# A hybrid attention and pooling layer on one core: a second buffer for the output weights' pieces, and other places for three kinds of small steps

## The chip, the core and the metric

The kernel runs on one core of a Trainium2 chip. The metric is the device time of one execution in microseconds; the time before is the median of three runs, 1445.88 us. One more execution was profiled, and all rows of a profile that are shown come from it. The engines are named as the profile names them: PE multiplies matrices (its weight loads are PEld), DVE does elementwise work and reductions, ACT copies and applies functions, POOL is a slower elementwise engine, and SP only issues transfers. SP and POOL issue nearly all DMA transfers here, each from a queue of its own that is worked off in order.

## The reference

The layer takes x (1024 tokens by 2048 channels) and does, in float32:

```
h = x @ w_in + b_in                       # 2048 -> 4352 columns: q, k, v, g_attn, u_pool, g_pool
a = banded_sink_attention(q, k, v) * silu(g_attn)   # 16 heads of 64, 2 key heads, window 128,
                                          # blocks of 128 queries against 256 keys,
                                          # with a bias by distance and a learned sink per head
b = multiscale_pool(u_pool) * silu(g_pool)          # trailing means over 2, 4, 8, 16 tokens, a map per group
mix = concat(a, b) @ w_out                # 2048 -> 2048
ple = sigmoid(x @ w_gate_ple) * (p @ w_ple)
out = layer_norm(2 ** 0.25 * x + mix + ple)         # gain and bias per channel
```

## The kernel before, in words

**Products.** All large products run as three matmuls in a reduced float format (`mm3`, lines 180 to 185: high part times high part, high times low, low times high). A *job* makes two blocks of 128 output columns, for one half of the inner dimension of 2048. It uses seven products instead of eight (p1 to p7, line 47), on sums and differences of quarters of the weights and of the activations. One product is 12 matmuls of 128x512: 4 chunks by three. The weights of a job come as two raw pieces of 512 KB into a ring of five buffers (`raw`, `feed_raw`, line 194). For each product ACT casts a quarter to its high part (`wh`, line 816) and DVE takes the low part (`wl`, `lo`, line 131), up to four products ahead.

**Gathering.** Products accumulate in PSUM banks `qa` and `qb`, two buffers each. In a job that runs alone the order is p1, p2, p6, p5, p7, p3, p4 (operands b11, b21, t2, t1, t3, b22, t4). p1, p6, p7 and p4 share one `qa` bank, so that what a product left there has to be read before a later one may add to it: ACT copies it out (`part`, line 423) or DVE adds it (`part`, line 425). Only the product between the two covers that reading.

**Stages.** Stage 1 makes q, k, v from the first half of the inner dimension, stage 2 (from about 150 us to 700 us) from the second, and then the second half of all other columns. The attention runs inside stage 2, beside the products. Stage 3 takes the first half of the other columns and applies the gates, stage 4 and 5 are the output projection, and the layer norm ends the kernel.

**Places.** After each product the clock of the program moves by one *tick* (`tick`, line 162). Small steps are put at ticks: `after(n, step)` places a step n ticks from now, `later(n, step)` does so too, and besides puts its instructions, on each engine, behind the last gathering that was placed there. A planner with costs of its own then settles the order on each engine, and an engine never leaves that order. So the places set what stands in front of what on PE, ACT, DVE, POOL and SP.

**Attention.** `heads` (line 575) handles four heads and two blocks of 128 queries; sixteen such units start 9 ticks apart. Counted from its start, a unit loads queries and its two bias tiles at 0 (`s<-q`, `s<-in_rel`, line 593), splits the queries at 3, makes scores at 6 and 10 (`score`: 8 matmuls of line 613, then 4 reductions on DVE, line 616), the shift at 9 and 13, exponentials at 10 and 14, their scaling at 12 and 16, transposes at 15 and 19 (`trans`, line 649, one `tr` bank), and products with the values at 21 and 25 (`value`: 4 matmuls of line 665 into a `pv` bank, a copy on ACT, line 669, and two additions on DVE, line 672). Its tiles come from a pool of 15 buffers of 2 KB per partition (`slots0`, line 1285).

**Centring the output weights.** Beside all this `centre_weights` (line 937) loads the output weights twice in 64 pieces of 256 KB into `cw`, a pool of one buffer (line 1087). In the first pass DVE reduces each piece to sums (`wsum`, line 950), in the second it subtracts the mean (line 960) and SP stores the piece (`wc<-cw`). A piece is fetched at its tick and used two ticks later; the next one is fetched in that same tick, behind the use.

**End of stage 3.** The activations for stage 4 are split in seven steps (`make_pooled`, line 1337): each casts two tiles of 128x1024 on ACT and takes their low parts on DVE. The sixth (operand b22) is placed at tick 28, the seventh (t4) at 31.

Of the kernel before, what the change touches and what calls it, by code (L numbers as in the profile page):

```python
# [24 lines left out]
F32 = mybir.dt.float32  # L25
# [6 lines left out]
P = 128  # L32
T = 512
H = 4 * P
# [31 lines left out]
class Layer:  # L66
# [203 lines left out]
    def two(self):  # L270
        return self.tile(self.twos, [P, 2, self.F], "two")
# [303 lines left out]
    def heads(self, h, j, half):  # L575
# [9 lines left out]
        def begin():  # L585
            f = slice(h * T + 256 * half, h * T + 256 * half + 256)
            q = self.slot()[:, :T]
            rq.append(q)
            for i in range(2):
                self.load(two(q)[:, i], self.qd[j + i][:, f])  # L590
            for i in range(2):
                bias.append(self.slot()[:, :T].rearrange("p (e k) -> p e k", e=2))
                self.load(bias[i], self.rel[j + i])
# [82 lines left out]
                    self.load(self.pre[j + i][:, f], pre[0][:, i])  # L676

        begin()
        self.later(3, split)
        for n in range(2):  # L680
            for i in range(2):
                self.after(6 + 4 * n, lambda n=n, i=i: score(n, i))
            self.after(9 + 4 * n, lambda n=n: shift(n))
            self.after(15 + 4 * n, lambda n=n: trans(n))
            for i in range(2):
                self.after(10 + 4 * n, lambda n=n, i=i: softmax(n, i))
                self.later(12 + 4 * n, lambda n=n, i=i: share(n, i))
            self.after(21 + 4 * n, lambda n=n: value(n))


    def gate_ahead(self, j):
# [245 lines left out]
    def centre_weights(self, at, by):  # L937
# [2 lines left out]
        cells = [(b, h) for b in range(NB) for h in range(2)]  # L940
        sums = self.fix.tile([P, 8, NB], F32, name="wsum")
        mean = self.fix.tile([P, 8], F32, name="wmean")
        now = []

        def fetch(b, h):
            now.append(self.load(self.tile(self.cw, [P, H], "cw"), self.wout[b, 0][:, h * H : h * H + H]))

        def add_up(b, h):
            k = now.pop().rearrange("p (k m) -> p k m", k=4)
# [13 lines left out]
        for step in (add_up, centre):  # L963
            for c in cells:
                self.after(at, lambda c=c: fetch(*c))
                self.later(at + 2, lambda c=c, step=step: step(*c))
                at += by if step is centre and c[0] % 3 else 2
            if step is add_up:
                self.later(at + 1, take_mean)
                at += 2  # L970

    def split_total(self, total, w, cut):
# [50 lines left out]
    def norm_sums(self, sums, a, first, last):  # L1023

        for b in range(a.shape[-1] // P):
            self.nc.tensor.matmul(sums[:, b : b + 1], a[:, b * P : (b + 1) * P], self.ones[:, 0:1], start=first and b == 0, stop=last,
                                  skip_group_check=True)

    def norm_scale(self, L, wait=0):
# [55 lines left out]
    def run(self):  # L1085
        nc, tc, fix = self.nc, self.tc, self.fix
# [101 lines left out]
        parts, work, over = ExitStack(), ExitStack(), ExitStack()  # L1188
# [76 lines left out]
        self.turn.clear()  # L1265
        self.ident = fix.tile([P, P], F32, name="ident")
        make_identity(nc, self.ident)
        self.ones = fix.tile([P, P], F32, name="ones")
        nc.gpsimd.memset(self.ones, 1.0)
        self.mhalf = fix.tile([P, 8], F32, name="mhalf")  # L1270
        nc.gpsimd.memset(self.mhalf, -0.5)
# [10 lines left out]
        work = ExitStack()  # L1282
        self.new_part = lambda b: self.tile(pp, [P, 2, T], "part")
        self.slot_n = T
        self.slots = self.work_pool("slots0", 15, work)
        self.kv = self.work_pool("kv", 1, over)

        def build_kv(b, build, group, halves=(0, 1)):
# [24 lines left out]
        for i in range(n3):  # L1313
            if i == 1:
                over.close()
                work.close()
                work, over = ExitStack(), ExitStack()
# [6 lines left out]
            if i == n3 - 2:  # L1324
# [3 lines left out]
                work = ExitStack()  # L1328
# [6 lines left out]
                    self.after((1, 1, 5, 6)[n], lambda b=b: self.gate_ahead(b - GA0))  # L1335
                pooled()
                for n, step in enumerate(make_pooled):
                    self.after((10, 13, 16, 19, 22, 28, 31)[n], step)
                for n, b in enumerate(b for j in s3[-2:] for b in j.b):
                    self.after(16 + 2 * n, lambda b=b: self.gate_ahead(b - GA0))  # L1340
            first = self.groups[g + i][0][0]
# [28 lines left out]
        for i in range(n4):  # L1370
            if i == 1:
                work.close()
                work = ExitStack()
                at = next(i for i, p in enumerate(six) if p is not pp)
# [155 lines left out]
```

## Time and profile before

| what | us |
|---|---|
| three runs | 1445.77, 1445.88, 1448.65 |
| the profiled execution: its time | 1448.33 |
| its span, first to last instruction | 1446.6 |
| what lies around the span | 1.73 |
| PE busy | 1429.2 |
| DVE busy | 1115.5 |
| ACT busy | 792.1 |
| POOL busy | 232.8 |

[...] A row of the timeline gives start, duration, engine, line, operation, output, inputs, shapes, and in brackets how long the engine had been idle and on what it waited. A row of waits gives the total, the times and the longest.

### The profile page before, as it was taken

To read this page: it belongs to the slowest core of one execution; us is meant where nothing else is said; L and a number is where in the kernel's file an instruction comes from. 1 tells how busy PE (TensorE), PEld (TensorE's weight loads), DVE (VectorE), ACT (ScalarE), POOL (GpSimd) and SP (SyncE) were. 2 spreads that over 40 slices of the span, in tenths; PEclk is the share of its full clock that TensorE was granted. 3 is DMA by queue.
4 is the path that set the end of the run, shared out by engine and by line. 5 is a ranking of instruction groups with operands and counts; after the bars stand their busy time and mean duration, and the time that the engine had idled before them with its cause. 6 is when DMAs were issued, how large, how long until landed. Compare 5 with 4: busy or idle time off the path is not lost.

```text
span 1446.6 us, 20400 instructions
## 1 busy us (share of the span) xinstructions
PE 1429.2 (99%) x6820; PEld 1210.5 (84%) x6820; DVE 1115.5 (77%) x2045; ACT 792.1 (55%) x1565; POOL 232.8 (16%) x339
## 2 busy tenths in 40 slices
PE   9999999999999999999999999999999999999996
PEld 7888887888888888888888888888888888899996
DVE  6859567787788877878768876867678665987787
ACT  6546375665667656665664444443356433654476
POOL 0000202211122211212111211211001211111223
PEclk9999999999999999999999999999999999999998
DMA  9463877455456655566887869998699768494566
GB/s 358 180 240 120 233 204 225 154 180 177 159 192 200 206 176 184 196 212 211 219 248 210 227 206 287 343 274 266 193 303 308 218 179 232 131 280 111 118 238 228
DMA packets 119226, 311.86 MB, mean 216 GB/s; under 512 B 13585, under 2 KB 27281, under 8 KB 119121
## 3 DMA queue, kind: packets, MB, share of 16 engines
q1 hardware_dynamic: 94480, 230.08, 46.5%
q0 software_dynamic: 21312, 73.15, 21.4%
q10 hardware_dynamic: 3328, 7.34, 1.5%
q8 instruction: 53, 0.87, 0.2%
q14 instruction: 53, 0.43, 0.1%
HBM read 211.95 MB, written 98.57 MB: 215 GB/s over the span
## 4 chain that ended last, share of the span: by engine, by line
PE 90%; DMA 4%; issue 2%; DVE 2%; ACT 1%; POOL 0%; POOLq 0%; SPq 0%; DVEq 0%; ACTq 0%
PE qa L183 15%; PE qa L185 15%; PE qa L184 15%; PE qb L185 11%; PE qb L183 11%; PE qb L184 11%; DMA part<-r 2%; PE sc L613 2%; PE pv L665 2%; DMA cw<-in_wout 2%; PE sc L185 1%; PE sc L183 1%; PE sc L184 1%; PE tr L649 1%; DVE wl L126 0%
## 5 line engine op out<-in xcount | busy, mean ns | idle before, releaser
L816 ACT CAST wh<-raw 128x512 fp32r<-128x512 f32 x428 | 264.3, 619 | 402.9 <-PE qa L184 156.6
L126 DVE TENSOR_TENSOR wl<-raw,wh 128x512 fp32r<-128x512 f32 x428 | 295.2, 693 | 105.2 <-ACT wh L816 100.3
L423 ACT COPY part<-qa 128x512 f32<-128x512 f32 (+1 forms) x180 | 104.0, 578 | 83.9 <-PE qa L185 81.5
L126 DVE TENSOR_TENSOR part<-part,qb 128x512 f32<-128x512 f32 (+1 forms) x120 | 81.1, 676 | 45.2 <-PE qb L185 40.6
L183 PE MATMUL qa<-b11h,wh 128*128 128x512 f32 (+2 forms) x292 | 108.9, 373 | 0.4 <-ACT part L423 0.4
L183 PE MATMUL qb<-b21h,wh 128*128 128x512 f32 (+2 forms) x292 | 108.9, 373 | 0.0
L185 PE MATMUL qa<-b11h,wl 128*128 128x512 f32 (+2 forms) x292 | 108.7, 372 | 0.0
L185 PE MATMUL qb<-b21h,wl 128*128 128x512 f32 (+2 forms) x292 | 108.7, 372 | 0.0
L184 PE MATMUL qa<-b11l,wh 128*128 128x512 f32 (+2 forms) x292 | 108.6, 372 | 0.0
L184 PE MATMUL qb<-b21l,wh 128*128 128x512 f32 (+2 forms) x292 | 108.5, 372 | 0.0
L183 PE MATMUL qa<-t3h,wh 128*128 128x512 f32 (+1 forms) x260 | 100.5, 387 | 2.2 <-ACT part L423 2.2
L184 PE MATMUL qa<-t3l,wh 128*128 128x512 f32 (+1 forms) x260 | 100.3, 386 | 0.0
L185 PE MATMUL qa<-t3h,wl 128*128 128x512 f32 (+1 forms) x260 | 100.3, 386 | 0.0
L183 PE MATMUL qa<-t2h,wh 128*128 128x512 f32 (+1 forms) x260 | 100.1, 385 | 0.1
L183 PE MATMUL qb<-t1h,wh 128*128 128x512 f32 (+1 forms) x260 | 99.9, 384 | 0.0
L185 PE MATMUL qa<-t2h,wl 128*128 128x512 f32 (+1 forms) x260 | 99.8, 384 | 0.0
L183 PE MATMUL qb<-b22h,wh 128*128 128x512 f32 (+1 forms) x260 | 99.7, 384 | 0.0
L185 PE MATMUL qb<-t1h,wl 128*128 128x512 f32 (+1 forms) x260 | 99.7, 384 | 0.0
L185 PE MATMUL qb<-b22h,wl 128*128 128x512 f32 (+1 forms) x260 | 99.7, 383 | 0.0
L185 PE MATMUL qa<-t4h,wl 128*128 128x512 f32 (+1 forms) x260 | 99.7, 383 | 0.0
L183 PE MATMUL qa<-t4h,wh 128*128 128x512 f32 (+1 forms) x260 | 99.6, 383 | 0.0
L184 PE MATMUL qb<-t1l,wh 128*128 128x512 f32 (+1 forms) x260 | 99.6, 383 | 0.0
(336 smaller groups left out, 3494.3 us busy)
## 6 DMA issues: line engine op xcount, KB each, us to landing
raw<-in_win SPq DMA_DIRECT2D x65, 512.0 KB, 4.2
h<-part SPq DMA_DIRECT2D x34, 512.0 KB, 3.0
part<-h POOLq DMA_DIRECT2D x34, 512.0 KB, 6.6
cw<-in_wout SPq DMA_DIRECT2D x64, 256.0 KB, 3.0
raw<-in_wgate SPq DMA_DIRECT2D x32, 512.0 KB, 4.9
raw<-wc SPq DMA_DIRECT2D x32, 512.0 KB, 4.4
s<-in_x SPq DMA_DIRECT2D x44, 256.0 KB, 5.7
s<-in_rel SPq DMA_DIRECT2D x32, 256.0 KB, 4.3
```

Source lines behind the costliest of these rows:

```text
L126: return (eng or self.nc.vector).tensor_tensor(out=out, in0=a, in1=b, op=op)
L183: mm(ps, wh, xh, start=start, stop=False, skip_group_check=True)
L184: mm(ps, wh, xl, start=False, stop=False, skip_group_check=True)
L185: return mm(ps, wl, xh, start=False, stop=stop, skip_group_check=True)
L423: self.mark("ACT", self.nc.scalar.copy(out=dst, in_=ps))
L613: nc.tensor.matmul(ps[:, e, z:], q, kk[:, keys], start=k == 0, stop=k == 1)
L649: nc.tensor.transpose(ps[:, o : o + P], sc[n, i][:, e, P:], self.ident)
L665: nc.tensor.matmul(ps, w, t, start=i == 0, stop=i == len(ms) - 1)
L816: ins = self.nc.scalar.copy(out=out, in_=a)
```

## The change

There are five edits.

1. `centre_weights` has a second pool of one buffer, `cw2`, and takes the two in turn. A piece is still fetched every two ticks (later every two or three), but used three ticks after its fetch and no longer two. The pool of 2 KB buffers shrinks from 15 to 14, and the `ones` tile of 128x128 to 128x1.
2. In `heads` the products with the values move from ticks 21 and 25 to 19 and 24. 19 is the tick of the unit's second transposes and of the next unit's second scores; 24 is that of the next unit's first transposes and of the first scores of the unit after it.
3. The two bias tiles are loaded at tick 2 of a unit and not at 0.
4. Of `make_pooled`, the steps for b22 and t4 move from ticks 28 and 31 to 27 and 30, as `later` steps.
5. `norm_sums` takes the narrow `ones` tile as it is.

```diff
@@ heads
             for i in range(2):
                 self.load(two(q)[:, i], self.qd[j + i][:, f])
+
+        def masks():
             for i in range(2):
                 bias.append(self.slot()[:, :T].rearrange("p (e k) -> p e k", e=2))
                 self.load(bias[i], self.rel[j + i])
...
         begin()
+        self.after(2, masks)
         self.later(3, split)
...
-            self.after(21 + 4 * n, lambda n=n: value(n))
+            self.after(19 + 5 * n, lambda n=n: value(n))
@@ centre_weights
-        now = []
+        now, cws = [], [self.cw, self.cw2]
 
         def fetch(b, h):
-            now.append(self.load(self.tile(self.cw, [P, H], "cw"), self.wout[b, 0][:, h * H : h * H + H]))
+            cws.append(cws.pop(0))
+            now.insert(0, self.load(self.tile(cws[0], [P, H], "cw"), self.wout[b, 0][:, h * H : h * H + H]))
...
                 self.after(at, lambda c=c: fetch(*c))
-                self.later(at + 2, lambda c=c, step=step: step(*c))
+                self.later(at + 3, lambda c=c, step=step: step(*c))
                 at += by if step is centre and c[0] % 3 else 2
             if step is add_up:
-                self.later(at + 1, take_mean)
+                self.later(at + 2, take_mean)
                 at += 2
@@ norm_sums
-            self.nc.tensor.matmul(sums[:, b : b + 1], a[:, b * P : (b + 1) * P], self.ones[:, 0:1], start=first and b == 0, stop=last,
+            self.nc.tensor.matmul(sums[:, b : b + 1], a[:, b * P : (b + 1) * P], self.ones, start=first and b == 0, stop=last,
@@ run
-        self.ones = fix.tile([P, P], F32, name="ones")
+        self.ones = fix.tile([P, 1], F32, name="ones")
...
-        self.slots = self.work_pool("slots0", 15, work)
+        self.slots = self.work_pool("slots0", 14, work)
+        self.cw2 = self.work_pool("cw2", 1, work)
...
-                    self.after((10, 13, 16, 19, 22, 28, 31)[n], step)
+                    (self.later if n > 4 else self.after)((10, 13, 16, 19, 22, 27, 30)[n], step)
```

Three places show how this moves instructions. The first is DVE early in stage 2, where the first scores of the second unit are due. `wsum<-cw` is the reduction of a piece of the output weights, `s<-tr` the low part of transposed probabilities, the `L616` rows with `sc` are score reductions, and `wl` are low parts of weights. Before:

```order
L126 TENSOR_TENSOR wl_2164<-raw_1694,wh_2163 128x512
L126 TENSOR_TENSOR wl_2195<-s_493_2158,wh_2194 128x512
L950 TENSOR_REDUCE wsum<-cw_2153 128x4
L126 TENSOR_TENSOR wl_2241<-raw_1841,wh_2240 128x512
L126 TENSOR_TENSOR s_2221<-tr_2215,s_2220 128x512
L616 ISA s_2224,st_2024<-sc_2225,s_2028,cst 128x256
```

And with the change:

```order
L126 TENSOR_TENSOR wl_2166<-raw_1697,wh_2165 128x512
L126 TENSOR_TENSOR wl_2198<-s_493_2160,wh_2197 128x512
L126 TENSOR_TENSOR wl_2243<-raw_1844,wh_2242 128x512
L126 TENSOR_TENSOR s_2223<-tr_2217,s_2222 128x512
L618 ISA s_2226,st_2027<-sc_2227,s_2106,cst 128x256
...
L126 TENSOR_TENSOR part_2195<-part_2195,qb_2246 128x512
L954 TENSOR_REDUCE wsum<-cw_2155 128x4
```

The reduction that stood ahead of the low part and of the scores stands behind them now.

The second place is PE in stage 2, one product of a unit with the values (`pv`), among the products of a job. Before, it stands alone between two products of the job:

```order
L665 MATMUL pv_2732<-s_2518,v_437_1861 128x512
L665 MATMUL pv_2732<-s_2519,v_437_1861 128x512
L665 MATMUL pv_2732<-s_2522,d_438_1862 128x512
L665 MATMUL pv_2732<-s_2523,d_438_1862 128x512
L183 MATMUL qa_2697<-t2h_1385,wh_2633 128x512
```

With the change it stands ahead of transposes (`tr`) and scores (`sc`):

```order
L667 MATMUL pv_2651<-s_2532,v_437_1863 128x512
L667 MATMUL pv_2651<-s_2533,v_437_1863 128x512
L667 MATMUL pv_2651<-s_2536,d_438_1864 128x512
L667 MATMUL pv_2651<-s_2537,d_438_1864 128x512
L651 MATMUL tr_2661<-ident,s_2368 128x128 x2
L651 MATMUL tr_2661<-ident,s_2376 128x128 x2
L615 MATMUL sc_2685<-kh_1769,s_2436 128x256
```

So a unit's small matmuls interrupt the large products at two places of nine ticks and no longer at four.

The third place is ACT at the end of stage 3, where `b22h` and `t4h` are the casts for stage 4 and `part<-qa` are copies of finished products. Before:

```order
L816 CAST wh_10814<-raw_10760 128x512
L816 CAST b22h_11025<-two_10810 128x1024
L816 CAST b22h_11025<-two_10812 128x1024
L423 COPY part_10527<-qa_10534 128x512
L816 CAST wh_10837<-raw_10447 128x512
L816 CAST wh_10860<-raw_10760 128x512
L423 COPY part_10529<-qa_10557 128x512
```

And with the change:

```order
L819 CAST wh_10818<-raw_10764 128x512
L819 CAST wh_10841<-raw_10451 128x512
L423 COPY part_10531<-qa_10538 128x512
L819 CAST wh_10864<-raw_10764 128x512
L423 COPY part_10533<-qa_10561 128x512
...
L423 COPY part_10863<-qb_10994 128x512
L819 CAST b22h_11008<-two_10814 128x1024
L819 CAST b22h_11008<-two_10816 128x1024
L699 ACTIVATE part_10533<-part_10533,cst 128x1024
L423 COPY part_10860<-qa_10868 128x512
```

The casts of b22 no longer stand ahead of the copy of that `qa` bank; they follow some products later, ahead of another copy.

## The prediction

> **What bounds the kernel now.** I began with the busy times, then took PE's waits, then the stretches in which these waits lie, and last the timelines of the engines around them. First the page's busy times:
>
> ```profile
> PE 1429.2 (99%) x6820; PEld 1210.5 (84%) x6820; DVE 1115.5 (77%) x2045; ACT 792.1 (55%) x1565; POOL 232.8 (16%) x339
> ```
>
> PE is busy 99% of the span of 1446.6 us. The change takes no matmul away, so it can only win where PE stands still, runs at a lower clock, or loses time between matmuls. PE's waits by releaser (total, times, longest) name the places:
>
> ```profile
> PE qa L183 <- ACT part L423: 2.7, 2, 2.2
> PE sc L1054 <- POOL st L126: 1.1, 1, 1.1
> PE sc L613 <- DVE st L616: 0.3, 1, 0.3
> ```
>
> Two waits for a copy of a bank sum to 2.7 us; they are the only ones above half a microsecond between the kernel's start and its last steps. The stretches (length, busy time of PE, PEld, DVE, ACT, POOL with instructions, granted clock, DMA share, GB/s) show where:
>
> ```profile
> 234.00:236.70 2.70, 0.45 (x3) 0.05 (x1) 2.48 (x8) 2.70 (x11) 1.45 (x2) 1.00 0.85 246
> 236.70:240.00 3.30, 3.30 (x8) 2.63 (x9) 0.55 (x2) 2.98 (x4) 0.00 (x0) 0.52 1.00 241
> 242.00:640.00 398.00, 398.00 (x1910) 332.44 (x1909) 327.12 (x798) 248.65 (x639) 77.87 (x100) 1.00 0.55 186
> ```
>
> At 234 us PE stands, and afterwards its granted clock is 0.52. Over the 398 us that follow it never waits: nothing is to be won there but time between matmuls. PE's timeline gives the price:
>
> ```profile
> 204.65 0.39 PE L183 MATMUL qb<-b21h,wh 128*128 128x512 f32 x1
> 207.37 0.39 PE L183 MATMUL qa<-t2h,wh 128*128 128x512 f32 x1
> 234.01 0.39 PE L185 MATMUL qb<-t1h,wl 128*128 128x512 f32 x1
> 236.65 0.67 PE L183 MATMUL qa<-t3h,wh 128*128 128x512 f32 x1 [2.25 <-ACT part L423]
> 240.40 0.39 PE L183 MATMUL qa<-t3h,wh 128*128 128x512 f32 x1
> ```
>
> The first two rows are one product apart: 12 matmuls in 2.72 us, 0.227 each, which is the length of a tick. From 234.01 to 236.65 one matmul took 2.64 us, so 2.41 were lost. From 236.65 to 240.40 nine starts took 3.75 us where 9 x 0.227 = 2.04 would do: 1.71 us lost to the clock. Together 4.12 us.
>
> Why was the copy late? ACT's and DVE's timelines:
>
> ```profile
> 236.02 0.57 ACT L423 COPY part<-qa 128x512 f32<-128x512 f32 x1
> 233.43 0.21 ACT L625 ACTIVATE st<-st 128x4 f32<-128x4 f32 x1 [3.76 <-DVE st L126]
> ...
> 226.62 0.68 DVE L126 TENSOR_TENSOR wl<-s,wh 128x512 fp32r<-128x512 f32 x1
> 229.50 0.69 DVE L950 TENSOR_REDUCE wsum<-cw 128x4 f32<-128x512 f32 x1 [2.20 <-DMA cw<-in_wout]
> 230.70 0.68 DVE L126 TENSOR_TENSOR s<-tr,s 128x512 fp32r<-128x512 f32 x1
> ```
>
> The copy stands on ACT behind the exponentials, these behind the shift of the scores (ACT idle 3.76 us), the shift on DVE behind the score reductions, and these behind a reduction of output weights that waited 2.20 us for its piece. With one buffer the next piece is asked for only when the last is used up. The chain of waits shows two of these transfers and DVE's groups from 195 to 240 us the sum (idle time last):
>
> ```profile
> 216.82 6.39 DMA cw<-in_wout
> 223.95 5.53 DMA cw<-in_wout
> ...
> L950 DVE TENSOR_REDUCE wsum<-cw 128x4 f32<-128x512 f32 x7 | 4.8, 684 | 7.2 <-DMA cw<-in_wout 7.2
> ```
>
> A transfer of 5.5 to 6.4 us does not fit two ticks of 2.72 us, 5.44 us. DVE lost 7.2 us to these pieces there, more than PE then lost.
>
> **The change part by part.**
>
> *Second buffer, use after three ticks.* A piece now has three ticks, 8.16 us, and its fetch need not wait for the reduction before. The two transfers above fit. At this place the reduction stands behind the scores, so the 2.20 us go out of the path: the shift at 233.43 comes by that much earlier, the copy with its end at 236.59 ends by 234.4, against 234.24 when PE would want it. The waits before it in the same 7.2 us take the rest off. I book the pause and the slow clock as gone: 4.12 us. Bounds: 0, if the piece or another load is as late as before, and 4.12. The later waits for pieces (12.4 us in the second pass, by a row of waits given below) cost PE nothing now, since PE is busy through 398 us; I book 0, and they give DVE slack. The cover is DVE's lead of up to four products; without it they would cost their 12.4 us.
>
> ```profile
> DVE cw L126 <- DMA cw<-in_wout: 12.4, 10, 3.0
> DVE wsum L950 <- DMA cw<-in_wout: 8.9, 6, 3.6
> SPq L140 <- PE pv L665: 21.2, 8, 6.3
> ```
>
> *One slot fewer, bias tiles two ticks later.* Where no slot is free, a load waits on SP for the last reader of an old tile, and all that SP issues later waits too; the last row shows 21.2 us of such waits already. Behind them stand raw weight pieces and pieces of output weights. The bias is needed at tick 6, so four ticks or 10.9 us remain after tick 2, against a median of 4.3 us to land (the page's row for `s<-in_rel`, below). The values are taken up earlier, which frees their tiles earlier. I book 0; bounds -0.5 (the short wait at 651 us, 0.3 with its surroundings) and +6.3 once.
>
> ```profile
> s<-in_rel SPq DMA_DIRECT2D x32, 256.0 KB, 4.3
> ```
>
> *Products with the values beside other small matmuls.* The timeline of one such product:
>
> ```profile
> 276.10 0.39 PE L183 MATMUL qb<-b21h,wh 128*128 128x512 f32 x1
> 276.78 0.62 PE L665 MATMUL pv<-s,v 128*128 128x512 f32 x2
> 277.70 0.39 PE L183 MATMUL qa<-t2h,wh 128*128 128x512 f32 x1
> 278.39 0.40 PE L183 MATMUL qa<-t2h,wh 128*128 128x512 f32 x1
> ```
>
> From 276.10 to 278.39 there are ten matmuls, 2.29 us against 2.27 at 0.227: the interruption itself costs some 0.02 us. There are 32 of them (two in each of sixteen units), so at most 0.64 us is won if the merged groups add nothing, and nothing if they do. I take the middle, 0.3. What is moved lies otherwise beside the products: a copy of 64x512 on ACT (I take the 0.58 of a part copy, below) and two additions on DVE fall into a tick that has transposes and scores, which is the slow case below.
>
> *Steps for b22 and t4.* The second wait for a copy:
>
> ```profile
> 1107.48 0.39 PE L185 MATMUL qa<-t4h,wl 128*128 128x512 f32 x1
> 1108.28 0.50 PE L183 MATMUL qa<-b11h,wh 128*128 128x512 f32 x1 [0.41 <-ACT part L423]
> ...
> 1106.70 1.05 ACT L816 CAST b22h<-two 128x1024 fp32r<-128x1024 f32 x1 [2.62 <-DMA two<-cc]
> 1107.65 0.58 ACT L423 COPY part<-qa 128x512 f32<-128x512 f32 x1
> ```
>
> A cast waited for its transfer and the copy stood behind it: 0.80 - 0.23 = 0.57 us. In the new order that copy stands ahead, so 0.57 is won. The casts then stand after the copy at 1125.30 and ahead of one that PE needs before 1130.19:
>
> ```profile
> 1125.30 0.58 ACT L423 COPY part<-qb 128x512 f32<-128x512 f32 x1
> 1125.77 1.15 ACT L696 ACTIVATE part<-part,cst 128x1024 f32<-128x1024 f32 x1
> ...
> 1130.19 0.39 PE L183 MATMUL qa<-t3h,wh 128*128 128x512 f32 x1
> ```
>
> 1125.8 plus two casts (2.1), the gate (1.15) and the copy (0.58) is 1129.6: it fits by 0.6 us, and their data had landed when the cast at 1106.70 began. Bounds: +0.57 won and, if the gate's input is late by 1 us, 0.4 lost. The narrow `ones` tile changes neither count nor shape of PE's matmuls: 0.
>
> **Sum.** 4.12 + 0.57 + 0.3 = 5.0 us. Against the profiled execution's own time that is 1448.33 - 5.0 = 1443.3. That execution is 2.45 above the median, near the slowest of the three runs; the other two are within 0.11 of each other. Against the median the same sum gives 1440.9. If what the faster runs lack is the slow clock of 1.71, they can win only 3.3: 1442.6. I take 1442.4, near the last.
>
> **The clock.** The row for 236.70 to 240.00 shows 0.52 after a pause of 2.41 us. [...]
>
> **The rivals.**
>
> *The median run has only a short pause.* If the 2.45 us between profiled run and median are the slow clock (1.71) and a pause shorter by 0.74, the median run lost 1.67 there and wins 1.67 + 0.57 + 0.3 = 2.5: 1443.3. For it: the runs lie on two levels. Against it: nothing shows the pause of an unprofiled run.
>
> *The change doesn't do what it says.* From 225 us on the transfers are near their limit (DMA share 0.85 and 1.00 in the rows above), and the longest piece took 9.3 us, more than three ticks:
>
> ```profile
> 202.57 9.30 DMA cw<-in_wout
> ```
>
> Then DVE waits on, PE stops at another product, and only 0.57 + 0.3 is sure, with some 0.5 of the pause: 1445.88 - 1.4 = 1444.5. Against it: of the transfers shown it is the only one above 8.16 us, and a fetch no longer waits for the use of the piece before it.
>
> *Slower: bursts delay the turn of a bank.* One place now holds values, transposes and scores. DVE's four score reductions with the additions behind them, and PE's transposes and scores:
>
> ```profile
> 306.61 0.48 DVE L616 CUSTOM_DVE_ANT_0 s<-sc,s,cst 128x256 f32<-128x256 f32 x1 [1.89 <-PE pv L665]
> ...
> 308.43 0.85 DVE L126 TENSOR_TENSOR s<-pv,s 64x256 f32<-64x256 f32 x2
> ...
> 269.90 0.60 PE L649 MATMUL tr<-ident,s 128*128 128x128 f32 x4
> 271.30 0.39 PE L183 MATMUL qa<-b11h,wh 128*128 128x512 f32 x1
> ```
>
> From 306.61 to 309.28 this is 2.7 us, and with the low part of the transposes (0.68) 3.4, in a tick of 2.72 plus the group's own 2.3 (transposes and scores 269.90 to 271.30, 1.4; values 0.92). A copy or addition that must clear a bank within one product may come later by the added 0.58 + 0.85 = 1.4 us, and PE stops for it. It decides from the sixth such stop: 6 x 1.4 = 8.4 uses up the 5.0 and adds 3.4, 1449.3; with ten it is 1454.9. Four of the seven products have such a bank, so about 18 of the 32 groups could be hit. Against it: DVE was busy 327 of 398 us and no stop occurred; it also gets back its waits for pieces.
>
> **How the numbers follow.** Changes under about 0.2%, 2.9 us, cannot be told from none here: faster is below 1443.0, slower above 1448.8. Chances: the forecast 0.46 (its own range 1440.0 to 1443.3, mostly faster), the short pause 0.20 (1443.3, a third of it faster), the piece still late 0.18 (1444.5, same), bursts 0.16 (three quarters of it slower, the rest same by few stops). That gives faster 0.52, same 0.36, slower 0.12. The range goes from 1439.4 (1440.9 less the other half of the 0.64, the 0.5 at 651 us and the spread of the three runs downwards) to 1447.0, which holds the middle cases and a few bursts.
>
> **What would show it.** The wait at 234 us and the 0.52 in the clock are gone, and DVE's waits for `cw` fall from 12.4 + 8.9 = 21.3 us to below 5. The wait at 1108 us is gone and none appears at 1130. PE shows 32 merged groups and no waits for `part` copies from 242 to 640 us. I am wrong if PE's waits for `part<-qa` grow in stage 2, if score reductions wait for `s<-in_rel`, or if another stop of over 2 us with a low clock appears.

## The result, and the profile after

The changed kernel takes 1442.93 us (median of 7 runs, 1441.64 to 1444.13); the kernel before, beside it, 1446.4 (7 runs, 1445.77 to 1449.2). The recorded ratio is 0.9965, with a 95% interval from 0.9951 to 0.9979, which lies below 1: a small win, but a clear one. The prediction was 1442.4 with a range from 1439.4 to 1447.0. The profiled execution took 1442.94, its span is 1441.2 us against 1446.6. A second comparison with more runs (below, `g1_after`) gave 0.9979 (0.9971 to 0.9988). The medians differ by 3.5 and 2.8 us, and the ratios stand for 5.1 and 3.0, so the win is some 3 to 5 us.

The busy times of the changed kernel's page, then rows of PE's waits (total, times, longest):

```profile
PE 1426.2 (99%) x6820; PEld 1207.9 (84%) x6820; DVE 1113.1 (77%) x2045; ACT 792.2 (55%) x1565; POOL 239.5 (17%) x339
```

```profile
PE sc L1058 <- POOL st L126: 1.1, 1, 1.1
PE tr L551 <- ACT s L557: 0.6, 1, 0.6
PE pv L667 <- POOL s L658: 0.6, 2, 0.3
PE qa L183 <- ACT part L423: 0.4, 1, 0.4
PE qb L183 <- ACT part L423: 0.3, 1, 0.3
```

The 2.7 us for copies of `qa` banks have become 0.4, and that one is another stop (484 us). What is new is small: 0.3 for a copy at 174 us, 0.6 at 193 us, and two waits for the masked probabilities at 648 us. Between 1100 and 1135 us PE waits for nothing. The stretches that the prediction used (length, busy time of PE, PEld, DVE, ACT, POOL, granted clock, DMA share, GB/s):

```profile
234.00:236.70 2.70, 2.70 (x14) 2.23 (x13) 0.63 (x1) 2.04 (x4) 0.00 (x0) 1.00 0.95 369
236.70:240.00 3.30, 3.30 (x22) 2.91 (x21) 2.54 (x6) 1.79 (x3) 0.64 (x1) 1.00 0.70 287
242.00:640.00 398.00, 397.60 (x1908) 332.01 (x1907) 326.38 (x796) 249.44 (x642) 78.75 (x98) 1.00 0.56 187
```

The stop at 234 us is gone and so is the clock of 0.52: 36 matmuls start in these 6.00 us where 11 did. DVE's groups that use the pieces (idle time last) waited 12.4 and 8.9 us before:

```profile
L126 DVE TENSOR_TENSOR cw<-cw,wmean 128x512 f32<-128x512 f32 x32 | 23.8, 744 | 0.3 <-DMA cw<-in_wout 0.2
L954 DVE TENSOR_REDUCE wsum<-cw 128x4 f32<-128x512 f32 x32 | 21.7, 678 | 0.0
```

Laid beside each other product by product, the two profiled executions differ as follows. The changed one starts 1.0 us better by 52 us, where nothing was changed, and loses 1.2 us of it at 174 and 193 us, where each profile has another value (below). From 194 to 248 us it gains 4.1 us, the stop and the slow clock. It loses 0.55 at 484 us and 0.5 about 648 us, and gains 0.6 at 1108 us, 1.3 after that and 0.3 in small steps between. All in all it is 5.0 us ahead at the last product. So the sum of the prediction was met in this pair, but the experiments show that its largest term isn't what other executions of the old kernel lose, and that its cause was only half told.

### The profile page after: what moved, and what is told of

Its sections match the earlier page's. It is cut to its first block, busy times and chain, and to the rows that moved or that the text cites. A ratio compares the mean times of both kernels' runs of the same rounds, so it can differ in the third digit from the quotient of the medians.

```text
span 1441.2 us, 20369 instructions
## 1 busy us (share of the span) xinstructions
PE 1426.2 (99%) x6820; PEld 1207.9 (84%) x6820; DVE 1113.1 (77%) x2045; ACT 792.2 (55%) x1565; POOL 239.5 (17%) x339
## 4 chain that ended last, share of the span: by engine, by line
PE 53%; DVE 1%; POOL 0%; ACT 0%; issue 0%; POOLq 0%; DVEq 0%; ACTq 0%
PE qa L185 9%; PE qa L183 9%; PE qa L184 9%; PE qb L183 7%; PE qb L184 7%; PE qb L185 7%; PE sc L185 1%; PE sc L183 1%; PE sc L184 1%; PE pv L667 0%; DVE sq L126 0%; PE pv L1030 0%; PE qb L1011 0%; DVE d L126 0%; PE qa L1011 0%
## 5 line engine op out<-in xcount | busy, mean ns | idle before, releaser
L184 PE MATMUL qa<-t4l,wh 128*128 128x512 f32 (+1 forms) x260 | 99.5, 383 | 0.0
```

The source lines that it names most:

```text
L184: mm(ps, wh, xl, start=False, stop=False, skip_group_check=True)
```

## The experiments

The ratios are to runs of the kernel before that were made beside them (29 to 33 runs, medians 1446.7 to 1447.1; for the first two rows those of the section above). "Stops" is the sum of what PE's starts between 100 and 1250 us lose against their rhythm (0.227 us from one start to the next behind a matmul of 128x512, whose row shows 0.39 us; 0.12 behind one of 128x256, whose row shows 0.28), where 0.25 us or more is lost at once.

| kernel | median us | ratio, 95% interval | span us | stop at 234 us | stops us |
|---|---|---|---|---|---|
| before (first profile) | 1446.4 | 1 | 1446.6 | 2.41, clock 0.52 after | 3.45 |
| the whole change (first profile) | 1442.93 | 0.9965 (0.9951 to 0.9979) | 1441.2 | none | 2.75 |
| e4_before | 1447.26 | 1.0008 (0.9998 to 1.0019) | 1445.6 | 1.24 | 3.73 |
| e2_pooled | 1446.90 | 1.0000 (0.9989 to 1.0011) | 1445.2 | 1.11 | 3.88 |
| f2_values | 1445.80 | 1.0000 (0.999 to 1.001) | 1444.1 | 1.81 | 5.04 |
| e1_cw | 1444.64 | 0.9985 (0.9973 to 0.9997) | 1441.9 | none | 1.75 |
| f1_masks | 1444.58 | 0.9989 (0.998 to 0.9999) | 1442.0 | none | 1.37 |
| e5_nocw | 1442.79 | 0.9973 (0.9964 to 0.9981) | 1442.7 | none | 2.79 |
| e3_noval | 1442.98 | 0.9975 (0.9966 to 0.9983) | 1440.2 | none | 0.50 |
| e6_lead2 | 1443.88 | 0.9978 (0.997 to 0.9987) | 1440.7 | none | 1.51 |
| e8_nopooled | 1443.38 | 0.9982 (0.9973 to 0.999) | 1441.4 | none | 1.78 |
| g1_after | 1443.95 | 0.9979 (0.9971 to 0.9988) | 1442.2 | none | 3.31 |

### The kernel before, once more

No edit.

> The kernel before once more, for a second profile of the same program. If the low clock at 234 us belongs to each execution: the same pause of 2.2 to 2.4 us and a granted clock near 0.5 behind it. If it belongs to the slower of the two levels of time only (1448 to 1449 against 1445.8): a profile whose time is near the lower level has a pause without a low clock, or a pause below 1.7 us. The times themselves differ from those of the kernel before by less than 0.2%.

Its stretches at 234 us, and the matmul that ended the stop:

```profile
234.00:236.70 2.70, 1.61 (x8) 1.27 (x8) 1.28 (x4) 2.70 (x6) 0.72 (x1) 1.00 0.87 278
236.70:240.00 3.30, 3.30 (x22) 2.92 (x21) 1.77 (x3) 2.55 (x5) 0.62 (x1) 1.00 0.98 269
```

```profile
235.16 0.50 PE L183 MATMUL qa<-t3h,wh 128*128 128x512 f32 x1 [1.09 <-ACT part L423]
```

The same program stopped for 1.24 us and not 2.41 (1.09 of it the wait), and the clock stayed at 1.00. The 4.12 us that the prediction took from one execution are 1.24 in another. The other stops moved as well: 0.62 at 485 us, which the first profile did not have, 1.02 at 649 (0.47 there), 0.85 at 1106 (0.57 there).

### The second buffer alone

```diff
-        now = []
+        now, cws = [], [self.cw, self.cw2]
...
-                self.later(at + 2, lambda c=c, step=step: step(*c))
+                self.later(at + 3, lambda c=c, step=step: step(*c))
...
-        self.slots = self.work_pool("slots0", 15, work)
+        self.slots = self.work_pool("slots0", 14, work)
+        self.cw2 = self.work_pool("cw2", 1, work)
```

with the narrow `ones` tile; values, bias tiles and the steps for b22 and t4 as before.

> The kernel before with the second buffer alone (use after three ticks, 14 slots, narrow ones). If the single buffer made the pause at 234 us (the theory of the prediction): the pause of 2.4 us and the low clock behind it are gone, DVE waits for cw fall from 21.3 us to below 5, and the time falls by 2.5 to 4.1 us, to 1442.3 to 1443.9. If the places of the attention's steps made it (the rival), the pause stays and the time is within 1 us of 1446.4. If fewer slots cost something by themselves, SP's waits for PE grow above 21.2 us and the time falls by less than 2 us.

DVE's groups of this kernel:

```profile
L126 DVE TENSOR_TENSOR cw<-cw,wmean 128x512 f32<-128x512 f32 x32 | 24.5, 764 | 0.0
L951 DVE TENSOR_REDUCE wsum<-cw 128x4 f32<-128x512 f32 x32 | 21.8, 680 | 0.0
```

The buffer does what it was said to do: no piece is waited for, and the stop at 234 us is gone. It is a sufficient cure. SP's waits for PE fell from 21.2 us to 6.6, so the missing slot cost nothing there. The median of 1444.64 lies above the 1442.3 to 1443.9 that were expected, and the ratio of 0.9985 is less than the whole win.

### The whole change without the second buffer

```diff
-        now, cws = [], [self.cw, self.cw2]
+        now = []
...
-                self.later(at + 3, lambda c=c, step=step: step(*c))
+                self.later(at + 2, lambda c=c, step=step: step(*c))
...
-        self.slots = self.work_pool("slots0", 14, work)
-        self.cw2 = self.work_pool("cw2", 1, work)
+        self.slots = self.work_pool("slots0", 15, work)
```

with the wide `ones` tile.

> The whole change without the second buffer (one buffer, use after two ticks, 15 slots). If the single buffer made the pause: a pause of 1.5 to 3 us with a low clock stays near 234 us, and the time falls by at most 1 us (0.57 at the end of stage 3, about 0.3 from merged groups), to 1445.4 or above. If the places made it: no pause near 234 us, and a time near 1443.

```profile
L126 DVE TENSOR_TENSOR cw<-cw,wmean 128x512 f32<-128x512 f32 x32 | 22.9, 716 | 6.2 <-DMA cw<-in_wout 6.0
L953 DVE TENSOR_REDUCE wsum<-cw 128x4 f32<-128x512 f32 x32 | 21.8, 681 | 2.6 <-DMA cw<-in_wout 2.6
```

With one buffer there is no stop at 234 us either, and DVE waits 8.6 us for pieces where it waited 21.3. The ratio, 0.9973, is no worse than those of the whole change (0.9965 and 0.9979). So the buffer isn't needed for the win: another part of the change cures the same stop. Two moves could do it, of the bias tiles and of the values; that of the steps for b22 and t4 acts only at the end of stage 3.

### One move at a time

Bias tiles alone (`f1_masks`), and values alone (`f2_values`), each put into the kernel before:

```diff
+        def masks():
             for i in range(2):
                 bias.append(self.slot()[:, :T].rearrange("p (e k) -> p e k", e=2))
                 self.load(bias[i], self.rel[j + i])
...
+        self.after(2, masks)
```

```diff
-            self.after(21 + 4 * n, lambda n=n: value(n))
+            self.after(19 + 5 * n, lambda n=n: value(n))
```

> Of the whole change this kernel has one edit: the two bias tiles of a unit are loaded at tick 2 and not at 0. One buffer for the pieces of the output weights, values at ticks 21 and 25, the steps of b22 and t4 as before. The whole change without its second buffer also had no stop at 234 us, and DVE waited 0.49 us there for its piece and not 2.1 to 2.2. Theory M (the bias tiles were in the way: 512 KB less on the queue just ahead of the piece, so that it lands earlier): DVE's wait for the piece ahead of the scores at 228 us falls below 1 us, PE's wait for the copy of the bank at 234 us falls below 0.3 us, its waits for pieces from 21 to 25 us in all to about 10; ratio 0.998 to 0.999, as with the second buffer alone. Theory V (the values are what counts): the wait for the piece stays at 2 us, the stop at 1.1 to 2.4 us, ratio 0.999 to 1.001.

> Of the whole change this kernel has one edit: the products with the values at ticks 19 and 24 and not 21 and 25. Theory V: the values free their tiles earlier and leave PE, ACT and DVE a quieter tick at 228 to 236 us, the stop at 234 us falls below 0.3 us and the ratio is 0.998 to 0.999. Theory M: DVE's wait of 2 us for its piece and the stop of 1.1 to 2.4 us stay, and only what the merged small matmuls save is won (22 groups by 0.011, some 0.3 us): ratio 0.9995 to 1.0005. If bursts of small work cost something, waits for score or values' banks of 0.3 to 1 us appear between 242 and 640 us that the kernel before does not have.

With the values alone the stop stays, 1.81 us, and the ratio is 1.0000. New stops come between 242 and 640 us: 0.66 and 0.52 at 455 us, 1.11 at 600 and 0.41 at 616. With the bias tiles alone the stop is gone, and the ratio is that of the second buffer within its interval. How it comes about is seen on SP's queue and on DVE. The kernel before, first SP's issues, then DVE's reductions:

```profile
198.49 0.33 SPq L140 DMA_DIRECT2D cw<-in_wout  x1
198.87 0.90 SPq L140 DMA_DIRECT2D s<-q  x2
199.81 0.91 SPq L140 DMA_DIRECT2D s<-in_rel  x2
202.57 0.33 SPq L140 DMA_DIRECT2D cw<-in_wout  x1
```

```profile
211.90 0.69 DVE L950 TENSOR_REDUCE wsum<-cw 128x4 f32<-128x512 f32 x1 [3.63 <-DMA cw<-in_wout]
216.10 0.69 DVE L950 TENSOR_REDUCE wsum<-cw 128x4 f32<-128x512 f32 x1 [0.71 <-DMA cw<-in_wout]
223.24 0.69 DVE L950 TENSOR_REDUCE wsum<-cw 128x4 f32<-128x512 f32 x1 [0.61 <-DMA cw<-in_wout]
```

and the same of the kernel with the bias tiles moved:

```profile
197.94 0.33 SPq L140 DMA_DIRECT2D cw<-in_wout  x1
198.33 0.90 SPq L140 DMA_DIRECT2D s<-q  x2
202.03 0.33 SPq L140 DMA_DIRECT2D cw<-in_wout  x1
```

```profile
207.62 0.68 DVE L953 TENSOR_REDUCE wsum<-cw 128x4 f32<-128x512 f32 x1
212.38 0.68 DVE L953 TENSOR_REDUCE wsum<-cw 128x4 f32<-128x512 f32 x1
221.88 0.68 DVE L953 TENSOR_REDUCE wsum<-cw 128x4 f32<-128x512 f32 x1
225.47 0.69 DVE L953 TENSOR_REDUCE wsum<-cw 128x4 f32<-128x512 f32 x1 [0.27 <-DMA cw<-in_wout]
```

Before, the piece asked for at 202.57 stands behind two bias tiles of 256 KB issued at 199.81, and its reduction comes at 211.90 after a wait of 3.63 us. With one buffer each piece is asked for when the one before it is used up, so a delay can be handed on: the waits are 3.63, 0.71, 0.61 and at last the 2.20 that stood ahead of the scores. Without the bias tiles in front the piece is used at 207.62, and the piece ahead of the scores is late by 0.27 us; the next one, behind the scores, is late by 1.80 us at 232.38 and no stop follows. Taking away either the bias tiles or the single buffer suffices: that is shown by `f1_masks`, `e5_nocw` and `e1_cw`. How the delay travels is read from the rows.

It does not travel only as lost time. The piece ahead of the scores was issued at 222.56 us in `e4_before` and at 222.59 in `f1_masks`, but took 5.43 us in the one and 2.85 in the other. What differs in the rows is POOL's queue: its load of 512 KB (`part<-h`) went out 1.13 us ahead of the piece in the one and 0.22 in the other. In the eleven profiles in which the piece stands 0.79 to 1.13 us behind that load it took 5.23 to 5.84 us, and in the three in which it stands 0.21 or 0.22 us behind (`f1_masks`, `e5_nocw`, `e6_lead2`) 2.85 to 3.08. My reading is that with one buffer a wait of about 0.6 us for the piece before (0.48 to 0.82 in the four profiles with the stop) is enough to put the fetch on the wrong side; no edit tried this by itself.

The size of the stop goes with the transfer that was issued at about 202 us. It lasted 9.30 us in the first profile of before (stop 2.41). In the chain of waits of `f2_values` and of `e4_before` its rows are these, with stops of 1.81 and 1.24:

```profile
201.66 8.48 DMA cw<-in_wout
```

```profile
202.21 8.20 DMA cw<-in_wout
```

In `e2_pooled`, with a stop of 1.11, the issue at 202.43 and the reduction at 210.68 are 8.25 us apart. From the shortest to the longest of these the transfer grows by 1.1 us and the stop by 1.2 to 1.3, and in the longest case the clock falls on top of it. The wait right ahead of the scores is much the same in all four (2.06 to 2.25 us); what differs is the wait for this first piece, 2.54 to 2.83 us and in the longest case 3.63. Four profiles make this likely and do not show it.

`f1_masks` also bears out a step that the prediction could only argue: DVE still waits 13.1 us for pieces in the second pass, and PE loses nothing by it from 240 to 640 us. With 5.1 us in the first pass that makes 18.2, where about 10 were expected: the stop went although most of the waits stayed.

### Two ticks with two buffers

```diff
-                self.later(at + 3, lambda c=c, step=step: step(*c))
+                self.later(at + 2, lambda c=c, step=step: step(*c))
```

in the whole change, with the mean taken one tick earlier as well.

> The whole change with the second buffer, but each piece used two ticks after its fetch and not three. If the time that a piece has is what counts (transfers of 5.5 to 6.4 us against two ticks, 5.44), DVE waits again for pieces, 5 to 9 us in all with single waits up to 1 us, as without the second buffer in the whole change (8.6). If what counts is that a fetch no longer waits for the use of the piece before it, the waits stay below 2 us. With the bias tiles out of the way no stop at 234 us in either case, and the ratio that of the whole change within 0.0008.

```profile
L126 DVE TENSOR_TENSOR cw<-cw,wmean 128x512 f32<-128x512 f32 x32 | 23.4, 730 | 0.1
L954 DVE TENSOR_REDUCE wsum<-cw 128x4 f32<-128x512 f32 x32 | 21.7, 679 | 0.0
```

No piece is waited for, as with three ticks. Beside the whole change without its buffer (8.6 us of waits, two ticks as well) it shows that the gain is the fetch that no longer waits for the use of the piece before it; the third tick adds nothing that shows. My reading that a transfer of 5.5 to 6.4 us does not fit two ticks put the weight in the wrong place. With two buffers a fetch goes out one use earlier: the pieces issued at 222.48 and 224.40 us in this kernel were used at 229.99 and 237.56, after 7.5 and 13.2 us.

### The steps for b22 and t4

Alone in the kernel before (`e2_pooled`), and taken out of the whole change (`e8_nopooled`, the same line the other way round):

```diff
-                    self.after((10, 13, 16, 19, 22, 28, 31)[n], step)
+                    (self.later if n > 4 else self.after)((10, 13, 16, 19, 22, 27, 30)[n], step)
```

> The kernel before with the steps for b22 and t4 alone moved. By the prediction: PE's wait at 1108 us goes, 0.57 us, and nothing else changes: 1445.8 against 1446.4, which a run can hardly tell from no change; the trace tells it. Rival: the casts now stand ahead of another copy, and a wait of 0.4 us or more appears near 1130 us.

> The whole change without the move of the steps for b22 and t4. If that move is worth its 0.57 us (the wait at 1108 us, booked as won in the prediction), the wait for the copy at 1108 us is back with 0.4 to 0.6 us and the ratio to the kernel before is 0.0004 above that of the whole change, 0.9969 against 0.9965; the profiled span about 0.6 us longer. The rival (the wait only changes its place: with that move alone a wait of 0.5 us for a cast came at 1120 us, and the ratio was 1.0000): the wait at 1108 us is there and no other, and ratio and span are those of the whole change within 0.2 us.

The wait at 1108 us is gone wherever the steps were moved. But in five of the eight profiles with the move PE stops some products later, for 0.4 to 1.0 us; in `e2_pooled` and in the second profile of the whole change it waits there for a weight cast:

```profile
1121.12 0.47 PE L183 MATMUL qb<-t1h,wh 128*128 128x512 f32 x1 [0.48 <-ACT wh L816]
```

```profile
1118.99 0.47 PE L183 MATMUL qb<-t1h,wh 128*128 128x512 f32 x1 [0.55 <-ACT wh L819]
```

These lose 0.64 and 0.71 us. Without the move the whole change loses 0.20 at 1103, 0.30 at 1115 and 0.18 at 1118 us, 0.68 in all: the wait for the copy did not come back with the 0.4 to 0.6 us that were expected, and in `f2_values`, where the steps were not moved either, it costs 0.1 us at most. The timed ratios, 1.0000 alone, and 0.9982 without against 0.9979 with it, tell no difference. By the traces the move is worth 0.6 us or so in some executions and nothing in others.

### The whole change without the values' new places, and once more whole

```diff
-            self.after(19 + 5 * n, lambda n=n: value(n))
+            self.after(21 + 4 * n, lambda n=n: value(n))
```

> The whole change with the products with the values back at ticks 21 and 25. The prediction books 0.3 us for the merged small matmuls, and holds a loss by bursts possible. If the merging saves what 22 groups at 0.011 us each make, the span is 0.3 us longer than that of the whole change and the ratio 0.9967 against 0.9965; the waits of 0.3 us twice for the masked probabilities at 647 to 650 us become one of 0.4, and the small stops at 174, 193 and 484 us stay. If the earlier values cost something (bursts), the stop at 484 us (0.55) goes and the span is 0.2 to 0.8 us shorter. A stop at 234 us would show that the values have part in its cure; I expect none.

> The whole change once more, beside the kernels that lack one part of it. Median ratio 0.9965 to 0.998, span 1440.8 to 1442. The stop at 234 us and a clock below 0.9 in stage 2 stay away in this second profile too, the waits at 174, 193, 484 and 647 us come again within 0.3 us of their sizes; the wait at 1108 us stays away.

Here a merged group of the first profile after:

```profile
324.59 0.63 PE L667 MATMUL pv<-s,v 128*128 128x512 f32 x2
325.05 0.63 PE L667 MATMUL pv<-s,d 128*128 128x512 f32 x2
...
326.91 0.40 PE L183 MATMUL qa<-t3h,wh 128*128 128x512 f32 x1
```

From 324.59 to 326.91 it takes 2.32 us. The two groups that it replaces took 1.40 (269.90 to 271.30) and 0.92 (276.78 to 277.70): the same. Over some 24 such groups the median saving is 0.014 us in `f2_values` against the kernel before, and 0.002 in the whole change against `e3_noval`. Against that stand the two waits at 648 us, which come since the values' masked probabilities are now asked for right behind their transposes, while POOL is still making them:

```profile
648.52 0.50 PE L667 MATMUL pv<-s,d 128*128 128x512 f32 x1 [0.29 <-POOL s L658]
...
649.56 0.50 PE L667 MATMUL pv<-s,d 128*128 128x512 f32 x1 [0.30 <-POOL s L658]
```

```profile
647.71 1.80 POOL L658 TENSOR_SCALAR_AFFINE_SELECT s<-s 128x512 fp32r<-128x512 f32 x2 [18.06 <-PE tr L651]
```

They lose 0.46 and 0.47 us, and the stop at 484 us loses 0.55. All three were there again in `g1_after` at the same sizes, in `e8_nopooled` and in `f3_hold` (the whole change with idle work added, below). `e3_noval` has none of them, one stop of 0.50 at 457 us instead, and the shortest span of all, 1440.2. The timed ratios, 0.9975 and 0.9979 in one comparison, can't be told apart. The values' move wins nothing that can be measured, and beside the other edits it costs about one microsecond by the traces. It isn't the only thing that can bring such stops: `e4_before` and `e2_pooled`, with the old places, also stop at 485 to 487 us, for 0.62 and 1.13 us, and these two and the first profile of before stop once at 650 to 652 us, for 0.47 to 1.02 us, there for score reductions. The stop at 193 us is the execution's: 0.77 in one profile of the whole change, 1.13 in the other, none of 0.25 or more in `e3_noval`, `e6_lead2` and `e8_nopooled`, 0.99 in `e5_nocw`; it goes with no edit. The stop at 174 us did not come again in `g1_after`, as I had expected it to.

### How long a stop must be for the clock to fall

Work that does nothing was added to the whole change: ACT copies a 128x128 tile many times at several ticks. In `f3_hold` it has no tie to its place; in `f4_hold`, whose edit follows, the next copy of a bank is issued behind it:

```diff
+        def hold(k):
+            for _ in range(k):
+                last = nc.scalar.copy(out=junk, in_=self.ident)
+            self.gather_behind.append(last.ins)
+
+        for n, k in enumerate((14, 18, 22, 26, 30, 34, 38, 42)):
+            self.later(48 + 14 * n, lambda k=k: hold(k))
```

> The whole change with work added that does nothing: at six ticks of stage 2 (56, 74, 92, 110, 128, 146 ticks after its start, so at about 345, 394, 443, 492, 541 and 590 us) ACT copies a 128x128 tile 10, 14, 18, 22, 26 and 30 times, at about 0.28 us each 2.8 to 8.4 us, so that copies of finished banks come late and PE stops for 0 to about 6 us, each time a little longer. This measures by itself from which length of a stop on the granted clock falls, and what that costs. Theory K (a stop of 2.4 us is enough, as at 234 us in the first profile): every stop above 2.4 us is followed by a stretch of 3 to 4 us at a clock near 0.5, none below 1.3 us is; each costs 1.7 to 1.9 us more than its stop. [...]

> The whole change with work added that does nothing, now tied to its place: at eight ticks of stage 2 (48, 62, 76 and so on to 146 ticks after its start) ACT copies a 128x128 tile 14, 18, 22, 26, 30, 34, 38 and 42 times, at 0.25 to 0.3 us each some 4 to 12 us, and the next copy of a finished bank is issued only behind them, so that PE stops for 0 to some 6 us, each time longer. It measures by itself how long a stop must be for the granted clock to fall, and what that costs. Theory K (a stop of 2.4 us is enough, as at 234 us in the first profile, and one of 1.1 to 1.6 is not): every stop above 2.4 us is followed by 3 to 4 us at a clock near 0.5, none below 1.6 us is; each slow stretch costs 1.7 to 1.9 us beside its stop. [...]

The first missed its aim: all 120 copies ran between 8.8 and 85.3 us, beside the first stages, since nothing held them in stage 2. The 36 us of ACT work (0.30 a copy) cost PE nothing that shows (span 1442.7). The second ran its 224 copies from 307 to 648 us. They are interleaved with other work in the order, and of 66.5 us of added ACT time PE lost little: the span is 1446.5 us, 4 to 5 more than in the two profiles of the whole change. The two longest stops and the stretches after them were:

```profile
455.83 0.66 PE L551 MATMUL sc<-ident,s 128*128 128x128 f32 x4 [1.10 <-ACT s L129]
...
648.88 0.50 PE L183 MATMUL qa<-b11h,wh 128*128 128x512 f32 x1 [1.09 <-ACT part L423]
```

```profile
455.70:459.00 3.30, 3.17 (x16) 2.65 (x17) 2.83 (x5) 3.25 (x11) 0.74 (x1) 1.00 0.24 81
...
649.00:652.30 3.30, 3.30 (x15) 2.62 (x16) 1.89 (x3) 1.93 (x5) 0.66 (x2) 1.00 0.64 238
```

Stops of 1.26 and 1.24 us, and the clock stays at 1.00. The same holds for the longest stop of the other profiles, 1.81 us in `f2_values`:

```profile
236.70:240.00 3.30, 3.30 (x22) 2.94 (x21) 1.76 (x3) 3.21 (x6) 0.00 (x0) 1.00 0.90 274
```

So here stops of 1.1 to 1.8 us left the clock alone, and the one of 2.41 was followed by the slow stretch. Longer stops were not produced.

The traces say more, though. The first profile's granted clock fell at 236.82 us, was back at 240.23, 3.41 us later, and fell once more at 1438.31, in the last steps of the kernel; that is 352 times 3.4133 us after the first fall. In each of the fourteen profiles the record of the clock begins with a change 4.6 to 9.4 us after the start and has a fall in these last steps, and the two lie 417, 418, 419 or 420 times 3.4133 us apart (420 in the first profile of before, 418 in that of the whole change), wherever PE's work stood. So in these records the changes lie on instants 3.41 us apart. Between such instants the rows read, in the first profile and then in `f2_values`, where no change was recorded there and the instants are counted back from the fall at 1432.88 (234.80 is 351 times 3.4133 us before it):

```profile
233.41:236.82 3.41, 1.16 (x6) 0.66 (x5) 3.19 (x8) 3.39 (x12) 1.45 (x2) 1.00 0.86 231
236.82:240.23 3.41, 3.41 (x9) 2.64 (x10) 0.66 (x2) 2.86 (x4) 0.00 (x0) 0.50 0.99 244
...
231.39:234.80 3.41, 2.14 (x10) 1.44 (x8) 3.13 (x12) 2.84 (x11) 1.31 (x2) 1.00 0.79 212
234.80:238.21 3.41, 3.03 (x13) 2.54 (x14) 0.69 (x1) 3.41 (x6) 0.14 (x1) 1.00 0.88 238
```

The stop of 2.41 us lay whole between two instants, PE was busy for 1.16 us of 3.41, and the clock fell. The stop of 1.81 us was cut by one, which left 2.14 and 3.03 us of work, and it did not fall. That the place of a stop among these instants counts beside its length fits these rows, and two stops do not show it. Nor do the rows show a border in that work: in the last steps, with smaller matmuls, the clock fell after such stretches with 2.15 us of it in `f2_values` and 2.34 in `f4_hold`. Whether a stop of 2.4 us that an instant cuts in the middle costs the clock stays open.

## Why the prediction came out right, point by point

**The stop at 234 us, 4.12.** Right for the pair of first profiles (4.1), too large for the others: 1.24, 1.11 and 1.81 us in three other profiles of kernels that still had the stop, and no slow clock. The rival "the median run has only a short pause" put 1.67 there, which is near what these profiles show. That the forecast came out near the measured time all the same is in part luck: it had been drawn towards the faster runs by leaving the slow clock out, and other things that were booked at nothing came in on the winning side, about 1 us of it in the last stage (last section).

**The cause, "one buffer".** This is the step that failed in part. The chain was followed back to the late piece and stopped there. Three transfers earlier, in a row that the prediction itself showed (202.57, 9.30 us), stood the origin: the bias tiles ahead of it on SP's queue. The edit's first effect came out as forecast (DVE's waits for pieces fell from 21.3 us to 0.2), but the third tick, on which the prediction put the weight, added nothing that shows.

**"Bias tiles two ticks later: 0".** Wrong: alone they give 0.9989, as much as the second buffer alone within the intervals. Since both cure the same stop, the two don't add up.

**The later waits for pieces, 0.** Right: with 13.1 us of them left in the second pass, `f1_masks` shows no stop from 240 to 640 us.

**b22 and t4, 0.57.** The wait is gone, but in five of eight profiles a stop of 0.4 to 1.0 us comes some ten to fifteen microseconds later; I had looked for it at 1130 us. The prediction counts this wait among those above half a microsecond; its row shows 0.41, and only what PE loses by it is 0.57. Not measurable in the times.

**Merged small matmuls, 0.3.** Mis-sized: the 0.02 us for an interruption was right in its order, but merging saves 0.014 of it at best and 0.002 in the whole change. In all that is 0.05 to 0.3 us, less than the 1.5 us that the whole change loses at its three small stops.

**Bursts.** Right in kind and too large in size: in the whole change three stops of about 0.5 us in stage 2, not six of 1.4, and two of them from POOL's masks, not from DVE or the banks. The third is a wait of 0.40 us for a copy at 484 us, so the sign "no waits for `part` copies from 242 to 640 us" failed by that one; `e4_before` and `e2_pooled` have it too, with the old places.

**The clock.** That the faster runs may lack the slow clock was right: it stayed at 1.00 after the three stops of 1.11 to 1.81 us and after those of `f4_hold`, and was 0.52 after the one of 2.41. By the rows above the longest two of these stops differ in the work that they left between two instants, 1.16 us and 2.14. What decides whether the clock falls no run shows.

**What is left.** Second buffer and bias tiles each win 1.6 to 2.2 us by their ratios, the other moves alone nothing, and combinations of these 2.6 to 3.9 (5.1 in the first comparison, of seven runs). By the traces against `e4_before`, whose stops in stage 2 add up to 2.9 us, the executions of the changed kernel are 2.0 to 2.1 us better from 195 to 813 us; they are 0.2 to 0.9 better from 813 to 1212 us, where the b22 steps lie; and about 1 us better from 1212 us to the last large product, for which the last section has rows. The few steps behind it are 0.6 to 0.9 us shorter than in `e4_before`; why was not looked into. That the combinations win more than their parts fits with this, but isn't settled by the intervals.

## What to carry to other kernels

Follow a late transfer back to the first one that was late, and look what was issued just ahead of it on the same queue: with one buffer the delay was passed on from piece to piece here (waits of 3.63, 0.71, 0.61 and 2.20 us), so that either a second buffer or moving a load out of the way cured it, and one must not book both. Look at the other queue as well: here the decisive piece took 5.2 to 5.8 us when it went out 0.79 to 1.13 us behind a load of POOL's, and 2.9 to 3.1 when 0.21 or 0.22 us lay between the two. Take the size of a stop from several profiles before it becomes the largest term of a sum; here it was 2.41 and 1.24 us in two profiles of one program, and only the longer brought the slow clock with it. Moving work off the place of one wait brought small new waits of about 0.5 us here, which have to be counted against the gain.

## What the runs showed that I had not expected

In the last stage the rhythm of the 128x384 matmuls depends on the program. Twenty matmuls of `e4_before`, then of `e1_cw` (first and twenty-first start of an unbroken series):

```profile
1329.80 0.34 PE L183 MATMUL qa<-t3h,wh 128*128 128x384 f32 x1
...
1333.29 0.34 PE L185 MATMUL qb<-b22h,wl 128*128 128x384 f32 x1
```

```profile
1327.05 0.34 PE L183 MATMUL qa<-t3h,wh 128*128 128x384 f32 x1
...
1330.52 0.34 PE L185 MATMUL qb<-b22h,wl 128*128 128x384 f32 x1
```

They take 3.49 and 3.47 us. Over some 670 such starts the mean is 0.1747 to 0.1751 us in before, `e4_before`, `e2_pooled`, `f1_masks` and `f2_values`, 0.1766 in `e5_nocw`, and 0.1735 to 0.1738 in all eight profiles with the second pool and the narrow `ones` tile. That is about 1 us for 670 matmuls. It was the same in both executions of each of the two programs that were profiled twice, and the edits add or remove no matmul; the prediction booked the `ones` tile at 0. These edits can move the addresses of other tiles; whether that is the cause was not tried.
